# TensorE's order in the MLP: the scheduler's, or the order in which the code emits

## The chip, the cores and the metric

The kernel runs on one core of a Trainium2 chip. The metric is the device time of one execution in microseconds (us); less is better. Engines are named as in the profile: PE is TensorE (PEld its weight loads), DVE is VectorE, ACT is ScalarE, POOL is GpSimd, SP is the queue that issues most DMAs.

## The reference

One layer of an encoder on 512 tokens of width 1024, in float32: a token mixer with two kinds of recurrent heads, a cross-attention over 256 memory tokens, and a squared-ReLU MLP, each added to the residual stream, and a final RMSNorm. The change lies in the last part:

```python
def squared_relu_mlp(xn, w_up, w_down):          # xn (512, 1024), w_up (1024, 4096), w_down (4096, 1024)
    return jnp.square(jax.nn.relu(xn @ w_up)) @ w_down
...
x = x + squared_relu_mlp(rmsnorm(x, norm_mlp[l]), w_up[l], w_down[l])
return rmsnorm(x, norm_final)
```

## The kernel before

Every float32 product is made of three matmuls (`mm3`, L225 to L227, and `product`, L1008 to L1010): each operand is split into a high part, which TensorE can multiply exactly enough, and a low part, the rest. The split is two instructions, a cast on ScalarE (L221, tiles `wh`) and a subtraction on VectorE (L222, tiles `wl`). Weights come by DMA into three `st` buffers, and there are three `wh` and three `wl` buffers, so the cast of one weight tile can begin only when TensorE has finished with the tile three before it.

The MLP runs over four blocks of 1024 hidden units, `for f in range(4)`, called passes here. In each pass:

- Eight up-projections (`proj_d("up", ...)`) of 24 matmuls each write one PSUM bank `mm`. VectorE applies relu and the norm's factor (L964), ScalarE squares. In pass 0 the first of them follows directly on the cross-attention: its operand `xT`, in two tiles of four blocks, is written by ScalarE (L773, high parts) and VectorE (L774, low parts), block after block, while TensorE already multiplies. In the same place `rms_row` has TensorE transpose the norm factors (L861, four small matmuls).
- The down-projection is done by a scheme with seven products P1 to P7 instead of eight, each in two halves g = 0 and 1 over the hidden units and two row blocks u = 0 and 1. Half of a product and one u is two times three matmuls of 512 columns. `JOBS` lists them: P1 g0, P2 g0, P1 g1, P2 g1, P6 g0, P6 g1, P5 g0, P5 g1, P7, P3, P4. `ahead` splits the weight tile of the job two further on.
- The products lie in three pairs of PSUM banks: X (`sm`: P1, then P6, P7 and P4 on top), Y (`mm`: P2), Z (`sm`: P5, then P3 on top). P6 accumulates onto P1 in X, but the residual takes a copy of P1 alone first: `add_to` (L935) reads X[0] and X[1] after P1's second half, so P6 must wait for these two adds. Z is empty when P5 starts, so P5 waits only for its weights.
- VectorE also makes the sums of weight tiles that the scheme needs (`early_sums`, L904 and L906, and `source`, L884).

The code emits instructions in the order in which it is written. Without further word, the framework's scheduler then decides the order within each engine, and may put a later instruction ahead of an earlier one. The built program holds one list for each engine, which it works through in that order, waiting where an input or a buffer is not ready. Instructions emitted under `tc.high_priority()` (weight splits) go first.

Of the kernel before, what the change touches and what calls it, by code (L numbers as in the profile page):

```python
# [77 lines left out]
def trunk(ctx: ExitStack, tc: tile.TileContext, x, mem, wpk, vec, cst, lmask, rmask, rows, out):  # L78
# [842 lines left out]
    def finish(t, r, first):  # L921

        o = 1 - first
        sc.activation(xr[t, first], xr[t, first], AF.Copy, scale=r)
        (nc.scalar if t == 3 else nc.sync).dma_start(out=out[t * P:t * P + P, first * 512:first * 512 + 512], in_=xr[t, first])
        z = xr[t, o]
        v.scalar_tensor_tensor(out=z, in0=z, scalar=r, in1=gfin[:, o * 512:o * 512 + 512], op0=ALU.mult, op1=ALU.mult)
        nc.sync.dma_start(out=out[t * P:t * P + P, o * 512:o * 512 + 512], in_=z)
# [4 lines left out]
    def add_to(t, c, ps, fin=False):  # L933
# [11 lines left out]
        r, _ = rstd_of(s1, 1, D)  # L945
        finish(t, r, pieces[t])

    for f in range(4):

        sta = []  # L950
# [175 lines left out]
```

## Time and profile before

| | us |
|---|---|
| median of 3 runs | 881.77 (881.75 to 882.56) |
| the profiled execution | 882.23 |
| its span, first to last instruction | 880.4 |
| TensorE busy | 855.4 (97%) |
| VectorE busy | 609.7 (69%) |
| ScalarE busy | 415.2 (47%) |

The MLP takes the stretch from about 536 us to the end; the first products of the passes' down-projections start at about 580, 663, 747 and 830 us. "Busy" counts the modelled length of a matmul, 0.39 us, though the next one starts 0.23 us later; for the cost of a matmul on the path the distance of starts counts. In the timelines a row is start, length, engine, line, operation, output and inputs (buffer numbers left out), and in brackets the idle time of the engine before it and what ended it. In the table of waits a row is who waited for whom, the sum in us, how often, and the longest.

### The profile page before, as it was taken

To read this page: it belongs to the slowest core of one execution; us is meant where nothing else is said; L and a number is where in the kernel's file an instruction comes from. 1 tells how busy PE (TensorE), PEld (TensorE's weight loads), DVE (VectorE), ACT (ScalarE), POOL (GpSimd) and SP (SyncE) were. 2 spreads that over 40 slices of the span, in tenths; PEclk is the share of its full clock that TensorE was granted. 3 is DMA by queue.
4 is the path that set the end of the run, shared out by engine and by line. 5 is a ranking of instruction groups with operands and counts; after the bars stand their busy time and mean duration, and the time that the engine had idled before them with its cause. 6 is when DMAs were issued, how large, how long until landed. Compare 5 with 4: busy or idle time off the path is not lost.

```text
span 880.4 us, 11056 instructions
## 1 busy us (share of the span) xinstructions
PE 855.4 (97%) x4198; PEld 709.1 (81%) x4198; DVE 609.7 (69%) x1038; ACT 415.2 (47%) x758; POOL 19.2 (2%) x50
## 2 busy tenths in 40 slices
PE   7999999999999999999999999999999999999995
PEld 5887888888887897888888888878887888788874
DVE  5457688779446987644554456797678758866885
ACT  5235443363357667544544346543444445435544
POOL 2000000010010000000000000000000000000001
PEclk9999999999999999999999999999999999999998
DMA  6432222312132333432221422404330432142002
GB/s 259 135 102 73 72 73 72 120 60 65 58 119 72 97 100 116 144 120 96 72 73 48 168 85 83 144 1 143 120 120 1 167 120 96 33 171 108 25 1 96
DMA packets 24615, 84.21 MB, mean 96 GB/s; under 512 B 2865, under 2 KB 2993, under 8 KB 24562
## 3 DMA queue, kind: packets, MB, share of 16 engines
q1 hardware_dynamic: 24272, 83.04, 27.7%
q8 instruction: 33, 0.54, 0.3%
q10 hardware_dynamic: 290, 0.47, 0.2%
q14 instruction: 20, 0.16, 0.1%
HBM read 81.40 MB, written 2.10 MB: 95 GB/s over the span
## 4 chain that ended last, share of the span: by engine, by line
PE 65%; DVE 2%; ACT 1%; POOL 0%; issue 0%; POOLq 0%; ACTq 0%
PE mm L226 14%; PE mm L227 14%; PE mm L225 14%; PE sm L1008 5%; PE sm L1009 5%; PE sm L1010 5%; PE sm L629 2%; PE sm L614 2%; ACT wh L221 1%; PE mm L1010 1%; PE mm L1009 1%; PE mm L1008 1%; PE sm L768 1%; PE sm L227 1%; PE sm L226 1%; PE sm L225 1%
## 5 line engine op out<-in xcount | busy, mean ns | idle before, releaser
L225 PE MATMUL mm<-xT,wh 128*128 128x512 f32 x552 | 219.5, 399 | 0.0
L226 PE MATMUL mm<-xT,wh 128*128 128x512 f32 x552 | 216.2, 392 | 0.2 <-DVE xT L774 0.2
L227 PE MATMUL mm<-xT,wl 128*128 128x512 f32 x552 | 216.1, 391 | 0.0
L222 DVE TENSOR_TENSOR wl<-st,wh 128x1024 fp32r<-128x1024 f32 x109 | 133.3, 1223 | 109.9 <-ACT wh L221 106.5
L221 ACT ACTIVATE wh<-st 128x1024 fp32r<-128x1024 f32 x109 | 115.4, 1059 | 183.7 <-PE mm L226 86.7
L227 PEld LDWEIGHTS mm<-xT,wl 128*128 128x128 f32 x552 | 103.6, 188 | 22.1 <-issue 0.6
L225 PEld LDWEIGHTS mm<-xT,wh 128*128 128x128 f32 x552 | 103.8, 188 | 21.5 <-issue 1.4
L226 PEld LDWEIGHTS mm<-xT,wh 128*128 128x128 f32 x552 | 103.8, 188 | 21.3 <-DVE xT L774 0.9
L1008 PE MATMUL sm<-wh,yT 128*128 128x512 f32 x128 | 49.9, 397 | 4.8 <-ACT wh L221 4.8
L227 PE MATMUL mm<-wh,yT 128*128 128x512 f32 x128 | 50.6, 395 | 0.0
L225 PE MATMUL mm<-wh,yT 128*128 128x512 f32 x128 | 50.4, 394 | 0.0
L226 PE MATMUL mm<-wl,yT 128*128 128x512 f32 x128 | 50.1, 391 | 0.0
L1009 PE MATMUL sm<-wl,yT 128*128 128x512 f32 x128 | 49.9, 390 | 0.0
L1010 PE MATMUL sm<-wh,yT 128*128 128x512 f32 x128 | 49.2, 389 | 0.0
L964 DVE SCALAR_TENSOR_TENSOR t<-mm,rg 128x512 f32<-128x512 f32 x32 | 22.1, 690 | 38.3 <-PE mm L227 38.3
L221 ACT ACTIVATE wh<-as 128x1024 fp32r<-128x1024 f32 x24 | 25.4, 1058 | 35.0 <-PE sm L1010 17.9
L935 DVE TENSOR_TENSOR vv<-sm,vv 128x512 f32<-128x512 f32 x48 | 31.9, 684 | 4.8 <-PE sm L1010 4.7
L1008 PEld LDWEIGHTS sm<-wh,yT 128*128 128x128 f32 x128 | 23.7, 188 | 12.6 <-ACT wh L221 6.5
L221 ACT ACTIVATE wh<-a 128x1024 fp32r<-128x1024 f32 x20 | 21.2, 1062 | 24.3 <-PE sm L1010 21.8
L222 DVE TENSOR_TENSOR wl<-a,wh 128x1024 fp32r<-128x1024 f32 x20 | 24.4, 1222 | 11.1 <-ACT wh L221 11.1
L376 PEld LDWEIGHTS sm<-a,t 128*128 128x128 f32 x224 | 30.1, 191 | 2.2 <-ACT t L366 0.4
L222 DVE TENSOR_TENSOR wl<-as,wh 128x1024 fp32r<-128x1024 f32 x24 | 29.4, 1223 | 3.2 <-ACT wh L221 3.0
(265 smaller groups left out, 1574.7 us busy)
## 6 DMA issues: line engine op xcount, KB each, us to landing
st<-in_wpk SPq DMA_DIRECT2D x109, 512.0 KB, 3.3
as<-in_wpk SPq DMA_DIRECT2D x16, 512.0 KB, 4.1
gate<-in_wpk SPq DMA_DIRECT2D x8, 512.0 KB, 4.3
a<-in_wpk SPq DMA_DIRECT2D x8, 512.0 KB, 4.9
as<-in_x SPq DMA_DIRECT2D x4, 512.0 KB, 6.4
vv<-in_x SPq DMA_DIRECT2D x8, 256.0 KB, 4.4
out<-vv SPq DMA_DIRECT2D x7, 256.0 KB, 2.2
a<-in_mem SPq DMA_DIRECT2D x2, 512.0 KB, 3.9
```

What stands on the lines that cost most here:

```text
L221: sc.activation(dst_hi, src, AF.Copy)
L222: v.tensor_tensor(out=dst_lo, in0=src, in1=dst_hi.bitcast(F32), op=ALU.subtract)
L225: pe.matmul(ps, lhsT=ah, rhs=bh, start=first, stop=False)
L226: pe.matmul(ps, lhsT=ah, rhs=bl, start=False, stop=False)
L227: pe.matmul(ps, lhsT=al, rhs=bh, start=False, stop=last)
L376: pe.matmul(ps[:, z], lhsT=kc[:, z], rhs=ap(q2, w * P, [2 * L, P // (2 * L)], [512 + L, 2], [1, L]), start=True, stop=True)
L614: pe.matmul(ps, lhsT=k[:, ws * P:ws * P + P], rhs=q, start=True, stop=True)
L935: v.tensor_tensor(out=z, in0=ps, in1=z, op=ALU.add)
L964: v.scalar_tensor_tensor(out=y, in0=ps, scalar=0.0, in1=rrow[:, 0:512], op0=ALU.max, op1=ALU.mult)
L1008: pe.matmul(ps, lhsT=ah, rhs=bh, start=new, stop=False, **fl)
L1009: pe.matmul(ps, lhsT=ah, rhs=bl, start=False, stop=False, **fl)
L1010: pe.matmul(ps, lhsT=al, rhs=bh, start=False, stop=end and k == 1, **fl)
```

## The change

For the rest of the kernel from the MLP on, TensorE's instructions are exempt from the scheduler: they stand in the order in which the code emits them. The other engines are still scheduled.

```diff
         r, _ = rstd_of(s1, 1, D)
         finish(t, r, pieces[t])
 
+    ctx.enter_context(tc.manual_schedule(engines={mybir.EngineType.PE}))
     for f in range(4):
 
         sta = []
```

Line numbers behind the added line are one higher in the changed kernel: L1008 becomes L1009. No instruction is added or removed. TensorE's order differs from the one before at five places: at the opening of pass 0, and once in each pass at the step from P2 to P6 and P5, in the same way each time. In the names below the first number is the tile's own, the same in both kernels; the second, from the allocation, is not.

TensorE, pass 0, end of P2 (`mm_854`), before. `sm_855` and `sm_856` are Z[0] and Z[1], for P5 with weights `wh_865`; `sm_851` and `sm_852` are X[0] and X[1], for P6 with weights 861/862 (g0) and 863/864 (g1):

```order
L1010 MATMUL mm_854_4956<-wh_859_4975,a4_845_4935 128x512
L1008 MATMUL sm_855_4957<-wh_865_5028,yT_800_4683 128x512
L1008 MATMUL sm_856_4958<-wh_865_5028,yT_800_4683 128x512
L1008 MATMUL sm_851_4953<-wh_861_4991,yT_800_4683 128x512
L1009 MATMUL sm_851_4953<-wl_862_4992,yT_800_4683 128x512
L1010 MATMUL sm_851_4953<-wh_861_4991,yT_800_4683 128x512
L1008 MATMUL sm_851_4953<-wh_861_4991,yT_817_4772 128x512
L1009 MATMUL sm_851_4953<-wl_862_4992,yT_817_4772 128x512
L1010 MATMUL sm_851_4953<-wh_861_4991,yT_817_4772 128x512
L1008 MATMUL sm_851_4953<-wh_863_5009,yT_835_4863 128x512
L1009 MATMUL sm_851_4953<-wl_864_5010,yT_835_4863 128x512
L1008 MATMUL sm_852_4954<-wh_861_4991,yT_800_4683 128x512
```

The same place now:

```order
L1011 MATMUL mm_854_4958<-wh_859_4977,a4_845_4937 128x512
L1009 MATMUL sm_851_4955<-wh_861_4993,yT_800_4685 128x512
L1010 MATMUL sm_851_4955<-wl_862_4994,yT_800_4685 128x512
L1011 MATMUL sm_851_4955<-wh_861_4993,yT_800_4685 128x512
L1009 MATMUL sm_851_4955<-wh_861_4993,yT_817_4774 128x512
L1010 MATMUL sm_851_4955<-wl_862_4994,yT_817_4774 128x512
L1011 MATMUL sm_851_4955<-wh_861_4993,yT_817_4774 128x512
L1009 MATMUL sm_852_4956<-wh_861_4993,yT_800_4685 128x512
```

The two matmuls of P5 that stood between P2 and P6 have gone back to P5's place, 24 matmuls on, and the two of P6 g1 that stood between X[0] and X[1] now follow X[1].

TensorE, opening of pass 0, before. `mm_786` is the first up block, `mm_793` the second; `xT_716` is the operand tile that is still being written; `sm_788` are the transposes of `rms_row`:

```order
L225 MATMUL mm_786_4597<-xT_716_4127,wh_765_4460 128x512
L225 MATMUL mm_793_4640<-xT_715_4126,wh_768_4490 128x512
L226 MATMUL mm_793_4640<-xT_715_4126,wh_768_4490 128x512
L227 MATMUL mm_793_4640<-xT_715_4126,wl_769_4491 128x512
L226 MATMUL mm_786_4597<-xT_716_4127,wh_765_4460 128x512
L227 MATMUL mm_786_4597<-xT_716_4127,wl_766_4461 128x512
L225 MATMUL mm_786_4597<-xT_716_4127,wh_765_4460 128x512
L226 MATMUL mm_786_4597<-xT_716_4127,wh_765_4460 128x512
L227 MATMUL mm_786_4597<-xT_716_4127,wl_766_4461 128x512
L225 MATMUL mm_786_4597<-xT_716_4127,wh_765_4460 128x512
L861 MATMUL sm_788_4625<-cs_67,tiny_781_4588 128x128
L226 MATMUL mm_786_4597<-xT_716_4127,wh_765_4460 128x512
```

The end of the same stretch now:

```order
L225 MATMUL mm_786_4599<-xT_716_4127,wh_765_4460 128x512
L226 MATMUL mm_786_4599<-xT_716_4127,wh_765_4460 128x512
L227 MATMUL mm_786_4599<-xT_716_4127,wl_766_4461 128x512
L861 MATMUL sm_788_4627<-cs_67,tiny_781_4588 128x128 x4
L225 MATMUL mm_793_4642<-xT_715_4126,wh_768_4490 128x512
L226 MATMUL mm_793_4642<-xT_715_4126,wh_768_4490 128x512
```

The first block now runs through without a break; the four transposes stand behind it, and then the second block begins with its first matmul.

VectorE, same place as the first pair, now. `vv_573<-sm_851` and `vv_574<-sm_852` are the adds that P6 waits for:

```order
L884 TENSOR_TENSOR a4_824_4814<-a4_824_4814,a4_850_4953 128x1024
L222 TENSOR_TENSOR wl_864_5012<-a4_850_4953,wh_863_5011 128x1024
L935 TENSOR_TENSOR vv_573_3213<-sm_851_4955,vv_573_3213 128x512
L222 TENSOR_TENSOR wl_866_5031<-as_787_4624,wh_865_5030 128x1024
L935 TENSOR_TENSOR vv_574_3215<-sm_852_4956,vv_574_3215 128x512
L935 TENSOR_TENSOR vv_573_3213<-mm_853_4957,vv_573_3213 128x512
L935 TENSOR_TENSOR vv_574_3215<-mm_854_4958,vv_574_3215 128x512
L222 TENSOR_TENSOR wl_868_5048<-gate_806_4722,wh_867_5047 128x1024
L935 TENSOR_TENSOR vv_577_3221<-sm_851_4955,vv_577_3221 128x512
L935 TENSOR_TENSOR vv_578_3223<-sm_852_4956,vv_578_3223 128x512
```

In passes 0 to 2 `wl_868` and `vv_577` have changed places (before, the add stood first); everything up to `vv_574<-mm_854` stands as before. ScalarE, GpSimd and the DMA queue have the same order as before.

## The prediction

> **What bounds the kernel now.** I read the page's busy table first, then TensorE's waits in the MLP, then the timeline around the one wait found there, engine by engine.
>
> ```profile
> PE 855.4 (97%) x4198; PEld 709.1 (81%) x4198; DVE 609.7 (69%) x1038; ACT 415.2 (47%) x758; POOL 19.2 (2%) x50
> PE sm L1008 <- ACT wh L221: 4.8, 4, 1.2
> ```
>
> The first row says that TensorE is busy 97% of the span. The second is the whole answer for TensorE's waits from 536 us on, that is over the MLP: one kind of wait, four times, 1.2 us each, once per pass of `for f in range(4)`. After each of them TensorE runs gapless to the next, so nothing downstream can absorb a delay: what TensorE loses in the MLP, the end loses.
>
> The place is the step from product P2 to P6 and P5. TensorE's own timeline in pass 0:
>
> ```profile
> 591.16 0.39 PE L1010 MATMUL mm<-wh,a 128*128 128x512 f32 x1
> 592.75 1.17 PE L1008 MATMUL sm<-wh,yT 128*128 128x512 f32 x3 [1.21 <-ACT wh L221]
> 593.76 0.40 PE L1009 MATMUL sm<-wl,yT 128*128 128x512 f32 x1
> 594.00 0.40 PE L1010 MATMUL sm<-wh,yT 128*128 128x512 f32 x1
> ...
> 594.70 0.39 PE L1010 MATMUL sm<-wh,yT 128*128 128x512 f32 x1
> 594.93 0.39 PE L1008 MATMUL sm<-wh,yT 128*128 128x512 f32 x1
> 595.16 0.40 PE L1009 MATMUL sm<-wl,yT 128*128 128x512 f32 x1
> ...
> 596.31 0.39 PE L1009 MATMUL sm<-wl,yT 128*128 128x512 f32 x1
> ```
>
> Columns are start, length, engine, line. A matmul's length is 0.39, but starts follow each other every 0.23 (594.70, 594.93, 595.16): 0.23 us is what one matmul costs on the path. The last of P2 starts at 591.16, so the next slot is 591.39. The row with x3 holds the two hoisted matmuls of P5 and the first of P6. The last row is the 15th matmul after the pause.
>
> At first sight the pause belongs to the hoisted P5: it waits for its weight cast on ScalarE. Whether P6 could have gone ahead is not in that row. It is in the weight loads and in VectorE's timeline:
>
> ```profile
> 592.75 0.30 PEld L1008 LDWEIGHTS sm<-wh,yT 128*128 128x128 f32 x2 [1.63 <-ACT wh L221]
> 593.42 0.19 PEld L1008 LDWEIGHTS sm<-wh,yT 128*128 128x128 f32 x1 [0.37 <-DVE vv L935]
>   DVE vv L935: 1.5, 4
> ```
>
> ```profile
> 580.71 0.69 DVE L964 SCALAR_TENSOR_TENSOR t<-mm,rg 128x512 f32<-128x512 f32 x1 [1.18 <-PE mm L227]
> 581.57 1.23 DVE L222 TENSOR_TENSOR wl<-gate,wh 128x1024 fp32r<-128x1024 f32 x1 [0.18 <-ACT wh L221]
> ...
> 590.40 1.22 DVE L884 TENSOR_TENSOR a<-a,a 128x1024 f32<-128x1024 f32 x1
> 591.54 1.22 DVE L222 TENSOR_TENSOR wl<-a,wh 128x1024 fp32r<-128x1024 f32 x1
> 592.67 0.69 DVE L935 TENSOR_TENSOR vv<-sm,vv 128x512 f32<-128x512 f32 x1
> 593.27 1.22 DVE L222 TENSOR_TENSOR wl<-as,wh 128x1024 fp32r<-128x1024 f32 x1
> 594.41 0.69 DVE L935 TENSOR_TENSOR vv<-sm,vv 128x512 f32<-128x512 f32 x1
> ```
>
> The first matmul of P6 also had to wait, for VectorE: 1.5 us in all over the four passes, by the third row of the upper fence. P6 accumulates on top of bank X, in which P1 lies, and P1 must first be read by the add of L935. That add of X[0] runs 592.67 to 593.36, and P6's load starts 0.06 later, at 593.42. The add of X[1] ends at 595.10. VectorE has had no idle time since 581.57 (the rows left out follow without a gap), and its last long idle time was ended by TensorE's up-projection at 580.71. So the adds are late by VectorE's backlog, and at a fixed distance behind TensorE. ScalarE's cast ends the pause only because P5 was put first; behind it VectorE's add sits 0.67 us later.
>
> **The change part by part.** *P5's two leading matmuls go back behind P6, in all four passes.* The wait for ScalarE goes. What is late next is the add of X[0]: VectorE's order up to it is the same row for row, so P6 starts at 593.42 as before, with the two P5 matmuls not done: 2 x 0.23 = 0.46 us lost. The time in which the old order did these two is idle in the new one.
>
> *P6's second row block is no longer preceded by two matmuls of P6 g=1.* In the new order six matmuls follow 593.42, at the times that the rows have: 593.42, 593.76, 594.00 to 594.70. The seventh opens X[1], is due at 594.93, and waits for the add that ends at 595.10, so it starts at 595.16. In the old order the matmul at 595.16 is the 10th: three behind is 3 x 0.23 = 0.69. After a pause the next step is 0.34, not 0.23 (593.42 to 593.76), because the weight load, too, starts only then: 0.11 more. Sum 0.80 us per pass. So the 15th starts at 595.16 + 0.34 + 7 x 0.23 = 597.11, against 596.31. The other passes have the same row:
>
> ```profile
> 592.75 1.17 PE sm L1008 x3
> ...
> 842.82 1.17 PE sm L1008 x3
> ```
>
> Four passes: 4 x 0.80 = 3.2 us.
>
> A rule bears on the 0.11. The Trainium skill, "TensorE: Matmul & The Clock Gate" (Part 2, step-by-step, LDWEIGHTS) says that TensorE's queue pulls weight loads ahead of matmuls in flight. Were P6's load pulled ahead of the wait, the pause would have no such tail and the total would be about 0.4 lower. The trace has the load of P6 at 593.42, behind the add, so I keep the 0.11.
>
> *At the start of pass 0, three matmuls of the second up block no longer fill a wait, and the four L861 transposes go behind the first block.* Rows of TensorE and of the VectorE ops that write the low halves of `xT`:
>
> ```profile
> 538.73 0.86 DVE L774 SCALAR_TENSOR_TENSOR xT<-sm,vc,xT 128x128 fp32r<-128x128 f32 x3
> 539.22 0.62 PE L225 MATMUL mm<-xT,wh 128*128 128x512 f32 x2
> 540.09 1.92 DVE L774 SCALAR_TENSOR_TENSOR xT<-sm,vc,xT 128x128 fp32r<-128x128 f32 x5
> 542.05 0.39 PE L225 MATMUL mm<-xT,wh 128*128 128x512 f32 x1
> 542.31 0.48 PE L226 MATMUL mm<-xT,wh 128*128 128x512 f32 x1
> 542.62 0.40 PE L227 MATMUL mm<-xT,wl 128*128 128x512 f32 x1
> 542.86 0.38 PE L861 MATMUL sm<-cs,tiny 128*128 128x128 f32 x2
> 543.31 0.39 PE L226 MATMUL mm<-xT,wh 128*128 128x512 f32 x1
> ```
>
> The first block needs VectorE's last two halves at 542.01 (540.09 + 1.92). In the new order TensorE comes to that matmul (the old 542.31) early, waits, and starts it at 542.07; the next, L227, at 542.07 + 0.34 = 542.41. Four L861 follow at about 0.11 each (two of them stretch two steps from 0.46 to 0.69 between 542.62 and 543.31). The second block's first matmul then starts at 542.41 + 0.23 + 0.44 = 543.08 and its second at 543.31. In the old order 543.31 is the fifth of that block. Three behind: 3 x 0.23 = 0.69 us.
>
> *VectorE, passes 0 to 2: the split of P5 g=1's weights moves ahead of the add of P6's X[0].* Cost nothing: both stand behind 595.10, and the new TensorE order reaches P5 g=1 only 36 matmuls after the pause, at about 602.2, and bank X again (P7) twelve later. Its weights' cast needs P6 g=0 finished (about 596.9), then 1.06 on ScalarE and 1.22 on VectorE: 599.2. That leaves 3 us of cover. ScalarE, GpSimd and the DMA queue keep their order; nothing else moves, and no instruction is added.
>
> Sum: 3.2 + 0.7 = 3.9 us slower. The profiled execution took 882.23 (span 880.4), which is 0.46 over the median of 881.77; it would become 886.1, and the median 885.7.
>
> **Bounds.** Low: only P6's first start counts, the add of X[1] no longer holds (0.46 x 4 = 1.8), and the opening costs nothing: 883.6. High: each of the two pauses costs 0.15 more, since steps after the pause are up to 0.24 instead of 0.23 (593.76 to 594.00) for a dozen matmuls: 4 x 1.1 + 0.7 = 5.1, or 886.9.
>
> **Rivals.** *(a) The pause simply goes.* If P1's adds were out of the way, P6 would start at 591.39 and the 15th matmul at 594.6, 1.7 earlier than 596.31: 4 x 1.7 - 0.7 = 6.1 us, 875.7. For it speaks the waits table, which names only ScalarE. Against it: the 0.37 of the weight load and VectorE's gapless backlog. It decides from where both adds come 0.97 us earlier than now (0.80 plus a quarter of 0.69): one 1.13 us op of L884 behind the add instead of ahead would do it. The new VectorE order has no such move, so 5%.
>
> *(b) The adds come earlier by part of that*, say 0.5 us, because VectorE loses less to the other engines: 4 x 0.3 + 0.7 = 1.9 at most, and without the opening 1.2: 883. Nothing on VectorE before 592.67 depends on what moves, so 8%.
>
> *(c) The longer pause lowers TensorE's rate.* In the first product at the kernel's start two matmuls in a row start 0.42 apart (13.31, 13.73), and that stretch, 11.01 to 15.10, is 4 us long; elsewhere the step is 0.23.
>
> ```profile
> 11.01 0.80 PE L225 MATMUL mm<-wh,xT 128*128 128x512 f32 x1
> ...
> 13.31 0.63 PE L225 MATMUL mm<-wh,xT 128*128 128x512 f32 x1
> 13.73 0.63 PE L226 MATMUL mm<-wl,xT 128*128 128x512 f32 x1
> ...
> 15.10 0.48 PE L225 MATMUL mm<-wh,xT 128*128 128x512 f32 x1
> ...
> 67.53 0.39 PE L226 MATMUL mm<-xT,wh 128*128 128x512 f32 x1
> 69.58 0.43 PE L554 MATMUL sm<-cs,a 64*128 64x64 f32 x4 [1.67 <-DVE a L543]
> ...
> 70.28 0.39 PE L225 MATMUL mm<-xT,wh 128*128 128x512 f32 x1
> 70.51 0.40 PE L226 MATMUL mm<-xT,wh 128*128 128x512 f32 x1
> ```
>
> Ten matmuls, as many as 4 us hold at that rate, would cost 10 x 0.19 = 1.9 us after each pause, 7.6 in all on top of the 3.9: 893.3. Against it: a pause from 67.53 to 69.58, start to start 2.05, was followed by steps of 0.23, and the new one is 2.26 (591.16 to 593.42). 3%. The same page of the Trainium skill (Part 1, "What's actually happening") has the clock halve after an idle window of about 3.4 us; by that rule, too, this pause is too short.
>
> **How the numbers follow.** My forecast 82%, (a) 5%, (b) 8%, (c) 3%, the rest for faults of size to either side. The likeliest is 885.7, its own range 883.6 to 886.9. With part of (b) the 8-in-10 range is 883.0 to 887.0. About 0.2% (1.8 us) is what a measurement can tell from no change: faster 6%, same 7%, slower 87%.
>
> **What would show it.** Right: four waits of TensorE at P6's first matmul, now put down to VectorE's add L935, of about 2.0 us, and a second, short one of about 0.2 before X[1]; the 15th matmul after the pause 0.8 later against the last of P2; a short wait for `xT` at the opening, with the second up block some 0.7 late. Wrong: P6 starting before the add of X[0] has ended, VectorE's adds at another distance from TensorE's last P2 matmul, or TensorE's step above 0.24 after the pause.

## The result, and the profile after

The changed kernel takes 891.82 us in the median of four runs (891.16 to 892.55) against 881.77 before: ratio 1.0109, 95% interval 1.0093 to 1.0125, 10 us slower. The forecast was 885.7 with a range to 887.0. The sign and the waits were right; the time was missed by 6 us, and those 6 us are not a wait. Line numbers are those of the changed kernel, one higher from the added line on.

The busy row of the page:

```profile
PE 862.5 (97%) x4198; PEld 713.9 (80%) x4198; DVE 609.2 (68%) x1038; ACT 415.2 (47%) x758; POOL 19.2 (2%) x50
```

The table of TensorE's waits over the MLP (sum, how often, longest):

```profile
PE sm L1009 <- DVE vv L935: 7.8, 4, 2.0
```

TensorE no longer waits for ScalarE at P5 but for VectorE's add of X[0] at P6, four times, 2.0 us at the longest. That is the wait that was forecast. VectorE, pass 0, shows its release:

```profile
594.57 0.68 DVE L935 TENSOR_TENSOR vv<-sm,vv 128x512 f32<-128x512 f32 x1
595.17 1.21 DVE L222 TENSOR_TENSOR wl<-as,wh 128x1024 fp32r<-128x1024 f32 x1
596.30 0.68 DVE L935 TENSOR_TENSOR vv<-sm,vv 128x512 f32<-128x512 f32 x1
```

The add of X[0] ends at 595.25, which is 2.21 us behind TensorE's last P2 matmul at 593.04; before it was 2.20 (593.36 against 591.16). VectorE's add has not moved against TensorE. TensorE there:

```profile
593.04 0.39 PE L1011 MATMUL mm<-wh,a 128*128 128x512 f32 x1
595.40 0.47 PE L1009 MATMUL sm<-wh,yT 128*128 128x512 f32 x1 [1.96 <-DVE vv L935]
595.70 0.40 PE L1010 MATMUL sm<-wl,yT 128*128 128x512 f32 x1
...
596.39 0.49 PE L1010 MATMUL sm<-wl,yT 128*128 128x512 f32 x1
596.68 0.63 PE L1011 MATMUL sm<-wh,yT 128*128 128x512 f32 x1
597.11 0.73 PE L1009 MATMUL sm<-wh,yT 128*128 128x512 f32 x1
...
599.76 0.49 PE L1009 MATMUL sm<-wh,yT 128*128 128x512 f32 x1
600.09 0.39 PE L1010 MATMUL sm<-wl,yT 128*128 128x512 f32 x1
```

After the pause TensorE first runs at its usual step. Then, from 596.68 to 599.76, a matmul is 0.63 us long instead of 0.39 and the step is 0.43 instead of 0.23, and at 600.09 all is as usual again. No engine and no transfer is waited for in that stretch. The view by windows gives the granted clock (the 1.00 or 0.50 ahead of the DMA share, the last two columns being DMA share and GB/s):

```profile
core 0: us, PE busy (x) PEld busy (x) DVE busy (x) ACT busy (x) POOL busy (x), PEclk, DMA share, GB/s
67.47:70.89 3.42, 1.74 (x11) 1.46 (x11) 3.37 (x5) 1.59 (x3) 0.00 (x0) 1.00 0.00 0
70.89:74.30 3.41, 3.41 (x10) 2.67 (x9) 3.17 (x5) 2.11 (x3) 0.00 (x0) 0.50 0.39 124
593.12:596.54 3.42, 1.46 (x7) 1.00 (x6) 3.42 (x5) 1.06 (x1) 0.00 (x0) 1.00 0.03 5
596.54:599.95 3.41, 3.41 (x10) 2.40 (x9) 1.64 (x3) 0.00 (x0) 0.00 (x0) 0.50 0.00 0
...
849.12:852.54 3.42, 1.46 (x7) 0.93 (x6) 3.42 (x4) 1.06 (x1) 0.00 (x0) 1.00 0.00 0
852.54:855.95 3.41, 3.41 (x9) 2.67 (x8) 3.22 (x6) 1.33 (x4) 0.00 (x0) 0.50 0.00 0
```

The bounds of these windows are the trace's own: each stretch at half clock begins and ends there, lasts 3.41 us, and the four of the MLP begin 85.33 us apart, 25 times 3.413. In the stretch of the same length ahead of each of these four TensorE was busy for 1.45 us of 3.41. The first pair is not in the MLP, and is called the early stretch below: it is the pause at L554 that the prediction quoted from the trace of before as harmless. In that trace it fell across the grid of windows in another way and went free:

```profile
66.10:69.50 3.40, 1.81 (x8) 1.13 (x7) 3.39 (x4) 2.21 (x3) 0.00 (x0) 1.00 0.00 1
69.50:72.90 3.40, 3.32 (x17) 2.78 (x18) 3.37 (x5) 1.58 (x2) 0.00 (x0) 1.00 0.00 0
```

By TensorE's starts row for row, the changed kernel is 0.40 us early against the kernel before ahead of that stretch and 1.24 late behind it, so it costs 1.64. Runs of one kernel fall into two groups that fit this: of 19 later runs of the kernel before, those at a mean clock of 0.996 or 0.997 took 881.84 to 882.58 (one 883.24), those at 0.995 882.95 to 883.48. That the longer ones were hit at this early pause is inferred: none of them was profiled. Medians below are given with the lowest run.

Counted by TensorE's starts: in pass 0 the 15th matmul after the pause begins 7.27 us after the last of P2 (at 600.32), 5.15 before. That is 2.12 lost, and 2.07 to 2.09 in the other three passes; 0.80 was forecast.

### The profile page after: what moved, and what is told of

It reads as the page before. It is cut to its first block, busy times and chain, and to the rows that moved or that the text cites. A ratio compares the mean times of both kernels' runs of the same rounds, so it can differ in the third digit from the quotient of the medians.

```text
span 890.7 us, 11063 instructions
## 1 busy us (share of the span) xinstructions
PE 862.5 (97%) x4198; PEld 713.9 (80%) x4198; DVE 609.2 (68%) x1038; ACT 415.2 (47%) x758; POOL 19.2 (2%) x50
## 4 chain that ended last, share of the span: by engine, by line
PE 60%; DVE 7%; ACT 1%; issue 0%; POOL 0%; POOLq 0%; ACTq 0%
PE mm L226 14%; PE mm L225 14%; PE mm L227 14%; PE sm L1009 4%; PE sm L1010 4%; PE sm L1011 4%; DVE wl L222 2%; PE sm L629 2%; PE sm L614 2%; ACT wh L221 1%; PE sm L768 1%; PE sm L227 1%; PE sm L226 1%; PE sm L225 1%; DVE yT L222 1%; DVE a L884 1%
## 5 line engine op out<-in xcount | busy, mean ns | idle before, releaser
L1009 PE MATMUL sm<-wh,yT 128*128 128x512 f32 x128 | 52.8, 412 | 7.8 <-DVE vv L935 7.8
L1010 PE MATMUL sm<-wl,yT 128*128 128x512 f32 x128 | 52.6, 411 | 0.0
L1011 PE MATMUL sm<-wh,yT 128*128 128x512 f32 x128 | 52.4, 409 | 0.0
L1009 PEld LDWEIGHTS sm<-wh,yT 128*128 128x128 f32 x128 | 25.4, 199 | 15.6 <-ACT wh L221 9.4
```

The costliest lines, as they stand in the source:

```text
L1009: pe.matmul(ps, lhsT=ah, rhs=bh, start=new, stop=False, **fl)
L1010: pe.matmul(ps, lhsT=ah, rhs=bl, start=False, stop=False, **fl)
L1011: pe.matmul(ps, lhsT=al, rhs=bh, start=False, stop=end and k == 1, **fl)
```

## The experiments

Two theories stood. One: the waits cost what the sum said (3.9 us), and the rest is TensorE at half clock, because it idled for too large a part of the window before. The other: the slow stretch belongs to the emitted order itself, P6 straight onto X[0] and X[1]. The place to read in each kernel is the step from P2 to P6.

### The pause filled with work that nobody uses

```diff
             w = ahead(n)
+            if n == 4:
+                spare = mmb()
+                for _ in range(8):
+                    pe.matmul(spare, lhsT=sta[0][p][0][:, 0:P], rhs=w[0][:, 0:512], start=True, stop=True)
             for u in range(2):
```

The two kernels that follow it here have 1 and 2 in place of 8.

> The changed kernel with eight extra matmuls of 512 columns in each pass, between the last of P2 and the first of P6, into a PSUM bank that nobody reads. They fill 8 x 0.23 = 1.8 of the 2.0 us for which TensorE waits there for the add of X[0]; P6 still waits for that add, at the same time as before. Theory (idle time halves the clock: in the changed kernel the granted clock was 0.5 for 3.41 us after each of the four pauses): no half-rate stretch in the MLP, and what is left is my first sum, 0.8 per pass and 0.7 at the opening, so 885.7 (884.8 to 886.6). Rival (the low rate comes from the order itself, P6 straight onto X[0] and then X[1], and not from the idle time): the half-rate stretches stay, 891 to 892.

Measured: 886.09 us (lowest 885.72), ratio 1.0042 (1.0026 to 1.0059). The add of X[0], and TensorE in pass 0:

```profile
591.75 0.39 PE L1011 MATMUL mm<-wh,a 128*128 128x512 f32 x1
591.97 1.98 PE L1034 MATMUL mm<-wh,yT 128*128 128x512 f32 x8
593.26 0.69 DVE L935 TENSOR_TENSOR vv<-sm,vv 128x512 f32<-128x512 f32 x1
594.00 0.50 PE L1009 MATMUL sm<-wh,yT 128*128 128x512 f32 x1
594.34 0.39 PE L1010 MATMUL sm<-wl,yT 128*128 128x512 f32 x1
...
595.26 0.40 PE L1011 MATMUL sm<-wh,yT 128*128 128x512 f32 x1
595.74 0.50 PE L1009 MATMUL sm<-wh,yT 128*128 128x512 f32 x1
```

The same place by windows:

```profile
594.00:597.50 3.50, 3.42 (x14) 2.51 (x15) 2.88 (x4) 0.02 (x1) 0.00 (x0) 1.00 0.00 0
```

P6 starts 2.25 us behind the last of P2 (2.36 in the changed kernel), 0.05 after the add has ended at 593.95, so it still waits for the add; but the clock stays at 1.00, and 32 more matmuls make the kernel 5.7 us faster than the changed one. This decides for the idle time. The rows also show the two small terms of the sum by themselves: 0.34 from P6's first to its second matmul, and 0.48 before X[1]'s. The 15th matmul of P6 starts 5.92 to 5.94 us after the last of P2 in all four passes, 0.78 to 0.80 later than in the kernel before. The run of 887.22, at a mean clock of 0.995, had no idle time in the MLP to pay for, which speaks for the early stretch.

> The changed kernel with one extra matmul per pass, directly behind the last of P2, into a bank that nobody reads. It shortens the idle stretch of TensorE from 2.1 to about 1.9 us in one piece; P6 starts when it did. Theory (the clock is halved for a window of 3.41 us when more than about half of the window before it, 1.7 us, was idle): still at risk; a pass is hit when the stretch lies in one window, so runs between 885.8 (no pass hit) and 891 (all four), 1.3 us per hit, more than one run hit. Rival (only a pause of 2 us or more counts): 885.8 in every run that has no half-rate stretch ahead of the MLP.

> As with one extra matmul, but two: idle stretch about 1.65 us. Theory (half of a window, 1.7 us): no pass hit, 885.8 in every run, 1.3 more only for a half-rate stretch ahead of the MLP. Rival (the limit is lower, 1.4 to 1.6 us, and the kernel before with its 1.36 us was just safe): passes are hit, 887 to 891.

Measured: one extra matmul 885.88 (lowest 885.77), ratio 1.0039 (1.0024 to 1.0054); two extra 886.58 (lowest 885.69), ratio 1.0046 (1.0031 to 1.0061). With one extra matmul the pause looks like this:

```profile
591.96 0.39 PE L1034 MATMUL mm<-wh,yT 128*128 128x512 f32 x1
593.99 0.50 PE L1009 MATMUL sm<-wh,yT 128*128 128x512 f32 x1 [1.64 <-DVE vv L935]
```

By windows, the early pause and this one:

```profile
66.08:69.49 3.41, 1.73 (x8) 1.13 (x7) 3.40 (x4) 2.21 (x3) 0.00 (x0) 1.00 0.00 0
591.74:595.15 3.41, 1.77 (x8) 1.18 (x7) 3.41 (x5) 1.06 (x1) 0.00 (x0) 1.00 0.00 0
```

A single matmul, 0.23 us of work, is enough: no run of it was hit in the MLP (mean clock 0.996 or 0.997), with the pause at 2.03 from start to start. My theory had expected some hits there. It was not the grid that spared it: in the trace the whole pause lies in one window in passes 0, 2 and 3, TensorE is busy 1.76 or 1.77 us of each, and the clock stays at 1.00. The limit lies between this pause and the 2.35 of the changed kernel. Two of the four runs with two extra matmuls (887.3 and 887.6, mean clock 0.995) have one stretch at half clock more than the others. They were not profiled; their pause is shorter than the one that went free with one extra matmul, so the early stretch is likelier than a hit in the MLP.

### One part undone: P5's matmuls first, by hand

```diff
             w = ahead(n)
+            if n == 4:
+                w5 = job(f, 6)
+                for u in (0, 1):
+                    pe.matmul(bank["P5"][u], lhsT=sta[0]["P5"][0][:, u * P:u * P + P], rhs=w5[0][:, 0:512],
+                              start=True, stop=False, skip_group_check=True)
             for u in range(2):
```

`product` does not repeat these matmuls later. The second kernel has `(0,)` in place of `(0, 1)`, one matmul instead of two.

> The changed kernel, TensorE still in emitted order, with the two leading matmuls of P5 written by hand ahead of P6 as the scheduler had put them; the two matmuls of P6 g=1 stay behind X[1]. This undoes one part of the change. Theory: the pause is cut into 1.36 us and some tenths, no half-rate stretch in the MLP; left are the second wait for the add of X[1] (one matmul behind, 0.23, and 0.11 for the late weight load, 0.34 per pass) and the opening (0.7): 881.8 + 4 x 0.34 + 0.7 = 883.8 (883.2 to 884.6). Rival (the low rate comes from the emitted order inside P6): half-rate stretches stay, 889 or more.

> The changed kernel with one of the two leading matmuls of P5 put ahead of P6 by hand. TensorE idles 1.36 us, runs that one matmul, and idles another 0.4: 1.8 us idle, broken in two. Unhit, it costs 0.7 at the opening and per pass 0.57 (two matmuls behind at the second wait, and 0.11), 881.8 + 3.0 = 884.8. Theory that the idle share of a window counts: some passes are hit, 1.3 us each, runs up to 889. Rival that only an unbroken pause counts (longer than 1.36): no run is hit in the MLP, 884.8 in all of them.

Measured: both ahead 885.38 (lowest 883.97), ratio 1.0026 (1.0017 to 1.0035); one ahead 885.02 (lowest 884.85), ratio 1.0034 (1.0021 to 1.0047). The wait is ScalarE's again:

```profile
PE sm L1035 <- ACT wh L221: 4.8, 4, 1.2
```

With both ahead, runs come in two groups: four of 883.97 to 884.27 at a clock of 0.996 or 0.997, and six of 885.25 to 885.83 at 0.994, above the range that was expected. The first group is 2.0 above the like runs of before, as worked out (0.7 + 4 x 0.34). In its trace the 15th matmul after the pause is 0.33 to 0.35 later than before in every pass, and the MLP has no half clock. The second group was not profiled; one early stretch would account for it. One ahead: three runs of 884.85 to 885.02, as worked out for no hit, and two of 886.1 and 886.3 at a clock of 0.995. The hits that the theory expected in the MLP did not come, in the trace at least. Its idle time, broken in two, was safe, but so was the one piece with one extra matmul, so this pair does not tell broken from unbroken.

### A long pause in two pieces

```diff
                 if g == 1:
+                    if p == "P1" and u == 0:
+                        v.tensor_copy(T2()[:, 0:512], bank[p][u])
                     for t0, c in into[p]:
                         add_to(t0 + u, c, bank[p][u], fin and p in last)
```

on top of the version with both matmuls of P5 ahead.

> The version with both leading matmuls of P5 put ahead of P6 by hand, and one extra copy on VectorE (X[0] to a buffer that nobody reads) ahead of the add of X[0]; with the split that then also goes first, P6 starts about 1.7 us later. TensorE idles 1.36 us, runs two matmuls, and idles another 1.8: 3.2 us idle, but the longest piece is no longer than the 1.8 us that was never hit with one extra matmul. Unhit: 882 + 0.7 + 4 x 1.73 = 889.6. Theory that the idle time of a whole window counts: passes are hit, granted clock 0.5 behind some pauses, 891 to 896. Rival that only an unbroken pause of 1.9 us or more counts: no hit in the MLP, 889.6.

Measured: 895.51 us (892.23 to 898.12), ratio 1.0151 (1.0117 to 1.0185); two of the four runs lie above the 896 that the theory allowed. The profiled run, of 893.84, has three windows at half clock, one behind the pause of pass 0 and two behind that of pass 3:

```profile
592.15:595.57 3.42, 1.05 (x4) 0.30 (x2) 3.42 (x5) 1.06 (x1) 0.00 (x0) 1.00 0.00 0
595.57:598.98 3.41, 2.91 (x7) 2.34 (x8) 2.24 (x4) 0.00 (x0) 0.00 (x0) 0.50 0.00 0
677.48:680.90 3.42, 2.13 (x9) 1.12 (x7) 3.42 (x5) 1.06 (x1) 0.00 (x0) 1.00 0.00 0
680.90:684.31 3.41, 1.82 (x8) 1.52 (x9) 3.32 (x5) 0.00 (x0) 0.00 (x0) 1.00 0.03 5
762.82:766.23 3.41, 1.84 (x7) 0.86 (x6) 3.41 (x5) 1.06 (x1) 0.00 (x0) 1.00 0.00 0
...
848.15:851.57 3.42, 1.56 (x6) 0.66 (x4) 3.42 (x4) 1.06 (x1) 0.00 (x0) 1.00 0.00 0
851.57:854.98 3.41, 2.40 (x6) 1.92 (x7) 3.22 (x6) 1.22 (x4) 0.00 (x0) 0.50 0.00 0
854.98:858.39 3.41, 3.41 (x10) 2.65 (x9) 0.84 (x2) 0.34 (x3) 0.00 (x0) 0.50 0.00 0
```

The stretches from 848.15 and from 592.15 were followed by half clock; those from 677.48, 680.90 and 762.82 were not. All hold parts of the same two pauses. What differs is how the grid cuts them: of these windows at full clock, TensorE was busy 1.05 and 1.56 us in those that were followed by half clock, 1.82 and more in those that were not. In the window from 848.15 no idle piece is long:

```profile
848.59 0.39 PE L1012 MATMUL mm<-wh,a 128*128 128x512 f32 x1
850.18 0.73 PE L1035 MATMUL sm<-wh,yT 128*128 128x512 f32 x2 [1.21 <-ACT wh L221]
852.58 0.80 PE L1010 MATMUL sm<-wh,yT 128*128 128x512 f32 x1 [1.67 <-DVE vv L935]
```

It holds 1.2 us of idle time, two matmuls, and the 0.7 us up to 851.57. The kernel before has that 1.2 us pause in every pass, and its trace shows no hit in the MLP. So it is the share of the window that counts, not the length of one pause, and the rival falls. In the MLP's windows at full clock, in all traces, the limit lies between 1.56 and 1.77 us busy of 3.41, about half. Busy time is not the exact measure, though: the early pause was hit at 1.74 in both profiles of the changed kernel, but not at 1.73 with one extra matmul, at 1.74 in the kernel of this section or at 1.81 before; and the window from 851.57, already at half clock, was busy for 2.40 and still followed by half clock.

Counting the work tells them apart. Take each 512-column matmul as 0.23 us from its start (0.43 at half clock), parts at the bounds by their share, smaller ones by their columns; fifteen fill a window at full clock. In the twelve traces, every window followed by half clock then holds at most 5.7, every other one at least 6.2: 5.2 from 851.57, 6.4 from 595.57. This limit of six is read off the traces after the fact; no kernel was made to test it.

### The opening alone

```diff
             a = []
+            opening = ExitStack()
+            if f == 0 and p == 0:
+                opening.enter_context(tc.manual_schedule(engines={mybir.EngineType.PE}))
             for j in range(2):
...
                 a.append(y)
+            opening.close()
```

> TensorE keeps the emitted order only in the first two up blocks of pass 0 (the opening); the rest of the MLP is scheduled as in the kernel before. Theory: 0.7 us for the three matmuls that no longer fill a wait: 882.5 (882.1 to 883.2). Rival: the opening carries part of the 10 us (the trace of the changed kernel is 1.9 late at the end of pass 0's P2, of which 1.2 I put down to a half-rate stretch at 71 us, before the MLP, that the kernel before did not have in its profiled run): then 883.5 or more.

Measured: 882.90 (lowest 882.41) beside 882.58 (lowest 881.84) of the kernel before, measured with it; ratio 1.0007 (0.9997 to 1.0016). By the interval alone that is no change; between the lowest runs it is 0.57, between the medians of the runs at a mean clock of 0.996 or more 0.62. Compared row by row, the changed kernel's TensorE is 1.21 late ahead of the moved matmuls in the trace, because of the early stretch (a matmul of the first up block at 540.43 against 539.22), and 1.88 late at the end of P2 (593.04 against 591.16), so the opening's own price is 0.67. In the trace of the opening alone the same two matmuls are 0.31 early (538.91) and 0.37 late (591.53): 0.68. There the wait for `xT` shows as single longer steps, 0.41, 0.33 and 0.29 instead of 0.23:

```profile
538.91 0.40 PE L225 MATMUL mm<-xT,wh 128*128 128x512 f32 x1
539.32 0.50 PE L226 MATMUL mm<-xT,wh 128*128 128x512 f32 x1
539.65 0.40 PE L227 MATMUL mm<-xT,wl 128*128 128x512 f32 x1
539.89 0.39 PE L225 MATMUL mm<-xT,wh 128*128 128x512 f32 x1
540.18 0.50 PE L226 MATMUL mm<-xT,wh 128*128 128x512 f32 x1
```

### The pause itself removed

```diff
         def ahead(n):
-            with tc.high_priority():
-                for m in range(n, n + 3):
+            for m in range(n, n + 3):
+                with tc.high_priority() if m not in (5, 6, 7) else ExitStack():
                     job(f, m)
```

> The kernel before (TensorE scheduled), with one other edit: the splits of jobs 5 to 7 (P6 g=1 and both halves of P5) are no longer emitted at high priority, so that VectorE takes the adds of X[0] and X[1] ahead of the split of P6 g=1 and of one L884 sum. By the durations of the trace the adds then end at about 591.1 and 591.7 instead of 593.36 and 595.10, so P6 follows P2 without a pause: 4 x 1.75 = 7.0 us less, 874.8 (874.0 to 876.5). Rival: VectorE's backlog only moves, and P6 g=1 or P5 waits for its low weights instead: 879 to 882.

Measured: 875.02 us (874.88 to 875.38), ratio 0.9914 (0.9899 to 0.9929), the fastest kernel of the study and 0.9% faster than the kernel before. VectorE in pass 0:

```profile
590.15 1.28 DVE L935 TENSOR_TENSOR vv<-sm,vv 128x512 f32<-128x512 f32 x2
591.35 1.21 DVE L222 TENSOR_TENSOR wl<-a,wh 128x1024 fp32r<-128x1024 f32 x1
```

TensorE at the same place:

```profile
590.90 0.39 PE L1010 MATMUL mm<-wh,a 128*128 128x512 f32 x1
591.13 0.39 PE L1008 MATMUL sm<-wh,yT 128*128 128x512 f32 x1
```

Both adds now run at 590.15 and are followed by the split; P6 follows P2 at the usual 0.23. The other half of the change is then tried on this version:

> The change made on top of the version whose VectorE adds come early (splits of jobs 5 to 7 without high priority; that version took 875.0). There P6 finds its adds done, so TensorE has no pause at that step in either order. Theory: the change then costs only the opening, 0.6 to 0.7 us: 875.7 (875.3 to 876.4). Rival (the emitted order is worse at other places of the MLP too): 878 or more.

Measured: 876.06 (875.83 to 876.38), ratio 0.9928 (0.9911 to 0.9944) to the kernel before. The emitted order costs 1.0 us here instead of 10. By the two traces the opening is 0.68 of it: the last matmul of P2 in pass 0 starts at 591.58 against 590.90, and the distance hardly changes up to pass 3 (836.41 against 835.75). There TensorE's weight load once waits for VectorE's split, which the matmul behind it pays with 0.44 instead of 0.23, and the rest of the 0.3 follows on the next steps:

```profile
845.23 0.19 PEld L1010 LDWEIGHTS sm<-wl,yT 128*128 128x128 f32 x1 [0.47 <-DVE wl L222]
```

### The changed kernel again

> The changed kernel once more, unchanged, for how often its passes are hit. Unhit it should take 885.9 (the versions with one or two extra matmuls in the pause took 885.9 with P6 starting at the same time); each half-rate stretch in a pass adds 1.3. Theory: a window of 3.41 us on a fixed grid is judged, so a pause of 2.1 us may fall across two windows and go free; but a hit pass lasts 85.4 us, 25.03 windows, so the pause of the next falls at the same place of the grid and is hit too. Runs then lie between 887 and 892.5, most at 891 or 892.5 (all four hit, without or with one ahead of the MLP). Rival (a pause of 2.1 us always costs): every run at 891.2 or 892.5.

Measured: 892.40 (892.19 to 892.76), ratio 1.0113 (1.0098 to 1.0128). Its profiled run has the half clock at 596.56, 681.89, 767.22 and 852.56, within 0.02 us of the first. All eight runs of the changed kernel lie between 891.1 and 892.8. The two profiled ones have five stretches at half clock, four of them in the MLP (mean clock 0.986); by their mean clock the runs at 0.988 have one fewer, and which one is not known. A hit pass lasts 85.4 to 85.5 us, little more than 25 windows, so the pause of the next falls near the same place of the grid; that fits all four being hit. That a run could also go unhit, as the theory says, was not seen, and these runs do not tell the two statements apart.

## Why the prediction was wrong

- *What bounds:* right. TensorE's order alone could not start P6; the add of X[0] released it, at the distance from P2 that the trace of before had.
- *The wait that goes and the one that comes:* right, 2.0 us four times for VectorE.
- *0.80 per pass:* right once the clock is kept up. In the three versions with extra matmuls the 15th matmul of P6 comes 0.78 to 0.80 later than before in every pass, and the runs at a mean clock of 0.996 or more take 885.7 to 886.4, for a forecast of 885.7. The second wait (0.48 instead of 0.23) and the late weight load (0.34) are in the rows of the filled pause.
- *The opening, 0.7:* 0.67 by the traces.
- *VectorE's swap at no cost:* nothing contradicts it; TensorE's waits in the MLP are for the add alone.
- *The step that failed is the rate of TensorE behind the pause.* The sum took the usual step of 0.23 there and put nothing for a slower one, which stood as rival (c) with 3%; what came is a step of 0.43 for 3.41 us in every pass, which is one of the forecast's own signs of being wrong (a step above 0.24). Rival (c) was dismissed on one pause of 2.05 us that was followed by the usual step, and on the rule of a whole idle window. The same pause was hit in the changed kernel's trace, and the two groups of run times of the kernel before fit that. One sample of an event that depends on where a fixed grid falls is no bound. The rows at the kernel's start, which I had quoted, showed that the low rate exists; its condition was read from too little.
- *Its price* was set at 1.9 us per pass, from ten slow matmuls. A stretch holds eight, 8 x 0.2 = 1.6, and 0.3 of that is the wait for X[1] that no longer shows, since TensorE comes later: 2.12 - 0.80 = 1.3. Sum: 0.7 + 4 x 0.8 + 4 x 1.3 = 9.1, of 10.05 between the medians and 9.4 between the lowest runs. The early stretch at 71 us, in the two longer of the four runs by their mean clock, is most of what is left of the 10.05; some 0.3 is not accounted for.

The Trainium skill, "TensorE: Matmul & The Clock Gate" (Part 1, "What's actually happening"), has the window right: it is free-running, 3413 ns long, and the clock is full or half; here 3.413 us, 1.00 or 0.50. It puts the fall after an idle window of about 3.4 us. Here 1.7 to 2.4 us of idle time in such a window, in one piece or two, were enough, and the measurement decides.

## What to carry to other kernels

A pause on TensorE has a second price behind it: if it leaves TensorE idle for about half of a 3.41 us window (here, fewer than six of the fifteen matmuls that fit), the next window runs at half clock. So in a kernel that TensorE bounds, look at the share of work in any 3.4 us around each pause before lengthening it, and treat a single pause that went free in one trace as no proof. When two orders differ in which engine ends a wait, ask what the later one is waiting behind: here taking VectorE's adds ahead of weight splits gained more (7 us) than either order of TensorE.

## What the runs showed of the hardware that was not expected

Half clock came in pieces of 3.413 us on one grid through a whole run, in the MLP of the changed kernel 25 windows apart. The same work, a pause of 2.05 us ahead of L554, was hit in two of the twelve profiled executions and not in the others, and cost 1.6 us in the first of the two, with nothing changed in the program up to there. One useless matmul per pass, 0.23 us of work, made the changed kernel 6 us faster.
